# The first tile of parameters loaded and used ahead of the others in a four-layer trunk, the rest through GpSimd's queue

## The chip, the cores and the metric

One core of a Trainium2 chip. It has five engines that run beside each other: TensorE (PE; weight loads shown as PEld), VectorE (DVE), ScalarE (ACT), GpSimd (POOL) and SyncE (SP), and 16 DMA engines that they share. The metric is the device time of one execution in microseconds (us), the median over runs.

## The reference

A trunk of four layers over 256 latent tokens `x` and 256 context tokens `ctx`, 1024 wide, float32. Each layer is a mixer (HGRN2, RWKV-7, latent attention, HGRN2) and a convolutional GLU, each behind an RMS norm with a shift, a scale and a gate that come from a conditioning vector:

```python
silu_c, silu_cc = silu(c), silu(c_ctx)
for layer in range(4):
    mod_l = split(silu_c  @ w_mod[layer] + b_mod[layer], 6)     # w_mod[layer]: 1024 x 6144
    mod_c = split(silu_cc @ w_mod[layer] + b_mod[layer], 6)
    h_l = rmsnorm(x_l, norm1[layer]) * (1 + mod_l[1]) + mod_l[0]
    ...                                                          # mixer, gate, norm2, conv-GLU, gate
```

For layer 0 the first matmuls of the mixer need h, which needs shift and scale (the first third of the modulation), which need silu of `c` and `c_ctx`.

## The kernel before, in words

The kernel is written as a program of tiles. A planner of the tile framework, at build time, gives each engine its own fixed order: it goes by the order of the program, but an engine that its own estimate has free takes later work that is ready. On the chip each engine then works strictly in that order and waits on semaphores. Tiles of one tag share a fixed number of buffers.

`trunk` (line 2200) calls `consts` (line 253: identity for transposes, masks, cleared and cut out on POOL), then each layer. `hgrn` (line 609) opens the pools of layer 0 and calls `start` (line 341) as a generator: up to its first `yield` it does the work around the change, and what is left of it (`yield from steps`) is worked off behind the first projection (line 644).

What `start` does before, in the order of the program:

- `load_x` (line 329): SP loads four tiles of 128 tokens (`it`, 512 KB each, line 334); per 128 channels PE turns four 128x128 blocks into a PSUM bank of the tag `S` (two buffers; line 338), DVE copies it to `xT` (line 339).
- `params` (line 281): 790 rows of 128 values (all small vectors of the model) are gathered into seven `stage` tiles of 128 rows by 28 DMAs from ACT's queue (line 317). Rows 0 to 127, the first tile, are exactly `c`, `c_ctx`, `norm1`, layer 0's `b_mod` and `norm2`: five DMAs. The other 23 fill tiles 1 to 6 (the other layers' `b_mod`, `hg_lb` in tile 2, the convolution's weights, the RWKV vectors and so on). Then each tile is turned on PE (line 322) and copied by DVE into `prm` (line 323). A stage tile is one of the 16 buffers of the tag `mraw` (line 625), which the `w_mod` tiles use too.
- `silu_c` (line 353): POOL clears `sc` (line 356), ACT applies silu to the columns of `c_ctx` and `c` (line 358; ACT loads a function table first).
- `lower_bounds` (line 570): a softmax over `hg_lb`, two Exp on ACT (lines 583, 584) and some ten small operations on DVE.
- `mod` (line 383): for each of three groups g, 32 `w_mod` tiles (128x512, 256 KB, SP, line 396), each multiplied with `sc` on PE (line 397, two instructions per tile, four row groups side by side in PSUM `at`); then a copy (`modev`, line 400), four transposes (line 403), and bias and norm gain on DVE (`mod_part`, lines 372 to 380). `start` takes five steps of it: all of the first group and the beginning of the second.

Behind it `norm_mod` (line 527) squares xT on ACT (line 508), adds three of the squares on POOL and others on DVE (line 512), sums over channels on PE (line 517), and makes h in pieces (DVE line 549, ACT line 551, DVE line 552). The projection loads `hg_w_in` in 512 KB tiles from SP (line 430, four buffers `wraw`), splits each into a high and a low part (ACT line 431, DVE line 432) and multiplies (lines 639 to 641).

DMAs from SP and ACT draw on one set of eight completion counters in the order planned: a DMA waits for the one that used its counter last. DMAs from POOL have eight of their own.

Of the kernel before, what the change touches and what calls it, by code (L numbers as in the profile page):

```python
# [122 lines left out]
class Jobs:  # L123
# [20 lines left out]
    def schedule(self, places, stage, lat, ordered, locks=(), eps=0.05):  # L144
# [48 lines left out]
        while len(order) < len(self.list):  # L193
            best = (math.inf,)
            for x in ready:
                t = start(x, best[0])
                if t is not None:
                    best = min(best, (math.floor(t / eps), x.place, x.index, t))
            x, t = self.list[best[2]], best[3]
            for y in x.takes:  # L200
                r = y["ring"]
                if r == ordered:
                    todo[int(x.pair)] -= 1
                if len(live[r]) >= self.rings[r]:
                    old = [i for i, o in enumerate(live[r]) if not o["left"]]
                    live[r][min(old, key=lambda i: live[r][i]["end"])] = y
                else:
                    live[r].append(y)
            end = ended(x, t) if x.engine == "PE" else t + x.cost
            free[x.engine] = end  # L210
            if x.engine == "Pool":
                port[0] = max(port[0], end)
            ready.remove(x)
            order.append(x)
            for y in x.takes + x.uses:
                y["left"] -= 1
                y["end"] = max(y["end"], end + x.lag)
            for y in x.then:
                y.at = max(y.at, end + x.lag + lat[x.engine, y.engine])
                y.need -= 1  # L220
                if not y.need:
                    ready.append(y)
# [3 lines left out]
class Trunk:  # L226
# [54 lines left out]
    def params(self, raw, psum):  # L281
        nc, a = self.nc, self.a
        rows = []

        def add(name, ap):
            rows.append((name, ap, ap.shape[0]))

        def flat(t):
            names = "abcd"[: len(t.shape)]
            f = t.rearrange(f"{' '.join(names)} -> ({' '.join(names)})") if len(t.shape) > 1 else t  # L290
            return f.rearrange("(r p) -> r p", p=P)

        add("c", flat(a["c"]))
        add("c_ctx", flat(a["c_ctx"]))
        add("norm1", flat(a["norm1"]))
        add("b_mod0", flat(a["b_mod"][0]))
        add("norm2", flat(a["norm2"]))
        for l in range(1, DEPTH):
            add(f"b_mod{l}", flat(a["b_mod"][l]))
        for n in ("hg_lb", "hg_norm", "ffn_conv", "ffn_conv_b", "rw_mu", "rw_w0", "rw_a0", "rw_k_k", "rw_k_a",  # L300
                  "rw_r_k", "rw_ln_w", "rw_ln_b", "mla_q_norm", "mla_kv_norm", "norm_f"):
            add(n, flat(a[n]))
        total = sum(r for _, _, r in rows)
        ntile = -(-total // P)
        self.prm = self.cst.tile([P, ntile * P], F32, name="prm")
        self.off = {}
        stage = [raw()[:, :P] for i in range(ntile)]
        if total % P:
            nc.vector.memset(stage[-1], 0.0)
        pos = 0  # L310
        for name, ap, r in rows:
            self.off[name] = pos
            done = 0
            while done < r:
                t, o = divmod(pos, P)
                n = min(P - o, r - done)
                nc.scalar.dma_start(out=stage[t][o:o + n, :], in_=ap[done:done + n, :])
                done += n
                pos += n
        for i in range(ntile):  # L320
            ps = psum()
            nc.tensor.transpose(ps[:, :P], stage[i], self.ident)
            nc.vector.tensor_copy(self.prm[:, i * P:(i + 1) * P], ps[:, :P])

    def col(self, name, i=0, n=1):
        o = self.off[name] + i
        return self.prm[:, o:o + n]
# [12 lines left out]

    def start(self, l, raw, xs, psum1, psum2):

        self.load_x(xs, psum2)
        self.params(raw, psum2)
        self.silu_c()
        self.lower_bounds()
        steps = self.mod(l, raw, psum1)
        for _ in range(5):
            next(steps)
        yield  # L350
        yield from steps

# [101 lines left out]
    def mm3(self, ps, wh, wl, xh, xl, start, stop):  # L454
        nc = self.nc
        nc.tensor.matmul(ps, lhsT=wh, rhs=xh, start=start, stop=False)  # L456
        nc.tensor.matmul(ps, lhsT=wh, rhs=xl, start=False, stop=False)  # L457
        nc.tensor.matmul(ps, lhsT=wl, rhs=xh, start=False, stop=stop)  # L458
# [1783 lines left out]
```

## Time and profile before

| | us |
|---|---|
| median of 3 runs (3150.14 to 3155.94) | 3151.34 |
| the profiled execution | 3154.18 |
| its span, first to last instruction | 3152.4 |
| TensorE busy in it | 2875.8 |

All stretches and times below are counted from the span's start. A busy time is the time in which an engine has an instruction; a row of a timeline may merge several instructions of one group (x26), and ends with the idle time before it and what ended that. "ACTq" and "SPq" are the queues of these engines, with the DMAs that they issue.

### The profile page before, as it was taken

Reading aid. Unit: us, or ns where it says so; the run is one execution under the profiler, and the core shown is the slowest. Engines: PE = TensorE matmul, PEld = TensorE weight load, DVE = VectorE, ACT = ScalarE, POOL = GpSimd, SP = SyncE. Lnnn points to the kernel's source line nnn. Section 1 sums busy time; section 2 is a strip of 40 time slices with the busy share of each in tenths; the row PEclk is TensorE's granted clock in tenths of the full one; section 3 lists DMA queues with packets and bytes.
Section 4 is the critical chain, followed back from the end, with each engine's and each line's share of the span. In section 5 each row is a group of like instructions: output and inputs, shape, how many; then the busy total and the mean of one; then the engine's idle time right before and its main releaser. Section 6 shows DMA issues by size and latency. Waiting matters only on the chain. (4 is left out here: it accounts for less than half of the span.)

```text
span 3152.4 us, 52606 instructions
## 1 busy us (share of the span) xinstructions
PE 2875.8 (91%) x20861; PEld 2292.2 (73%) x20861; DVE 1767.0 (56%) x3113; ACT 1391.1 (44%) x2642; POOL 552.2 (18%) x727
## 2 busy tenths in 40 slices
PE   7999999999787787788879999899899999999898
PEld 4588877778575556666658888776578887888898
DVE  4278765445573346866564444466554344488765
ACT  3266643334442145665543223345433233577544
POOL 1023322222442133444310000000000000123000
PEclk9999989999888888988779999899999998999999
DMA  8622168886756865666553332210123332332554
GB/s 282 197 68 68 52 220 269 282 283 221 223 178 200 235 194 156 172 173 182 166 169 94 100 94 91 76 41 30 54 80 101 94 94 80 87 94 77 155 185 127
DMA packets 475336, 452.70 MB, mean 144 GB/s; under 512 B 98492, under 2 KB 415826, under 8 KB 474962
## 3 DMA queue, kind: packets, MB, share of 16 engines
q1 hardware_dynamic: 458352, 398.27, 41.3%
q0 software_dynamic: 15360, 50.34, 4.8%
q8 instruction: 164, 2.69, 0.4%
q10 hardware_dynamic: 1378, 0.73, 0.1%
q14 instruction: 82, 0.67, 0.1%
HBM read 392.64 MB, written 56.10 MB: 142 GB/s over the span
## 5 line engine op out<-in xcount | busy, mean ns | idle before, releaser
L457 PE MATMUL mm<-hl,whi 128*128 128x512 f32 (+1 forms) x2024 | 744.9, 368 | 10.9 <-DVE hl L552 10.9
L456 PE MATMUL mm<-hh,whi 128*128 128x512 f32 (+1 forms) x2024 | 744.8, 373 | 10.3 <-ACT hh L551 6.9
L458 PE MATMUL mm<-hh,wlo 128*128 128x512 f32 (+1 forms) x2024 | 742.4, 368 | 0.0
L432 DVE TENSOR_TENSOR wlo<-wraw,whi 128x1024 fp32r<-128x1024 f32 (+1 forms) x392 | 464.7, 1188 | 428.9 <-ACT whi L431 415.6
L431 ACT CAST whi<-wraw 128x1024 fp32r<-128x1024 f32 (+1 forms) x392 | 395.9, 1013 | 554.0 <-PE mm L457 489.6
L456 PEld LDWEIGHTS mm<-hh,whi 128*128 128x128 f32 x2024 | 386.2, 192 | 91.1 <-issue 10.8
L457 PEld LDWEIGHTS mm<-hl,whi 128*128 128x128 f32 x2024 | 386.0, 191 | 79.2 <-DVE hl L552 14.4
L458 PEld LDWEIGHTS mm<-hh,wlo 128*128 128x128 f32 x2024 | 385.6, 191 | 66.1 <-issue 6.1
L456 PE MATMUL mm<-uh,whi 128*128 128x512 f32 (+1 forms) x704 | 255.2, 363 | 0.0
L457 PE MATMUL mm<-ul,whi 128*128 128x512 f32 (+1 forms) x704 | 255.1, 363 | 0.0
L458 PE MATMUL mm<-uh,wlo 128*128 128x512 f32 (+1 forms) x704 | 254.2, 363 | 0.0
L512 POOL TENSOR_TENSOR t<-t,t 128x512 f32<-128x512 f32 (+1 forms) x27 | 35.2, 1305 | 868.1 <-ACT t L508 866.8
L456 PEld LDWEIGHTS mm<-uh,whi 128*128 128x128 f32 x704 | 132.8, 189 | 24.1 <-issue 2.5
L457 PEld LDWEIGHTS mm<-ul,whi 128*128 128x128 f32 x704 | 132.9, 189 | 20.3
L458 PEld LDWEIGHTS mm<-uh,wlo 128*128 128x128 f32 x704 | 132.5, 189 | 20.6
L449 DVE TENSOR_TENSOR plo<-praw,phi 128x512 fp32r<-128x512 f32 x64 | 45.3, 709 | 171.4 <-ACT phi L448 171.3
L448 ACT CAST phi<-praw 128x512 fp32r<-128x512 f32 x64 | 39.8, 622 | 216.3 <-DMA praw<-in_rw_w_rkv_dram 119.7
L2128 DVE SCALAR_TENSOR_TENSOR t<-mm,prm,t 128x510 f32<-128x510 f32 (+1 forms) x88 | 60.0, 682 | 105.4 <-ACT t L2126 105.4
L566 DVE SCALAR_TENSOR_TENSOR xT<-mm,mod,xT 128x256 f32<-128x256 f32 x176 | 74.4, 478 | 67.2 <-PE mm L458 67.2
L2126 ACT ACTIVATE t<-mm,prm 128x512 f32<-128x512 f32 (+1 forms) x88 | 63.3, 719 | 108.2 <-PE mm L458 108.2
L725 POOL TENSOR_TENSOR t<-t 128x512 f32<-128x512 f32 x32 | 46.4, 1450 | 362.6 <-DVE t L715 319.3
L1889 PE MATMUL md<-mraw,sc 128*32 128x256 f32 x768 | 71.5, 449 | 29.6 <-DMA mraw<-in_w_mod_dram 29.3
(426 smaller groups left out, 5199.7 us busy)
## 6 DMA issues: line engine op xcount, KB each, us to landing
wraw<-in_ffn_w_in_dram SPq DMA_DIRECT2D x176, 512.0 KB
mraw<-in_w_mod_dram SPq DMA_DIRECT2D x192, 256.0 KB
mraw<-in_w_mod_dram SPq DMA_DIRECT2D x96, 512.0 KB
wraw<-in_hg_w_in_dram SPq DMA_DIRECT2D x80, 512.0 KB
wraw<-in_ffn_w_out_dram SPq DMA_DIRECT2D x80, 512.0 KB
ow<-preo SPq DMA_DIRECT2D x64, 256.0 KB
praw<-in_rw_w_rkv_dram POOLq DMA_DIRECT2D x48, 256.0 KB, 4.4
vw<-prev SPq DMA_DIRECT2D x32, 256.0 KB
```

The costliest lines, as they stand in the source:

```text
L431: nc.scalar.copy(h, r)
L432: nc.vector.tensor_tensor(out=w, in0=r, in1=h.bitcast(F32), op=ALU.subtract)
L448: nc.scalar.copy(hi, raw)
L449: nc.vector.tensor_tensor(out=lo, in0=raw, in1=hi.bitcast(F32), op=ALU.subtract)
L456: nc.tensor.matmul(ps, lhsT=wh, rhs=xh, start=start, stop=False)
L457: nc.tensor.matmul(ps, lhsT=wh, rhs=xl, start=False, stop=False)
L458: nc.tensor.matmul(ps, lhsT=wl, rhs=xh, start=False, stop=stop)
L566: nc.vector.scalar_tensor_tensor(out=self.xT[n][:, sl], in0=ps[:, sl], scalar=m[:, which * 8 + n, s:s + 1], in1=self.xT[n][:, sl], op0=ALU ...
L725: nc.gpsimd.tensor_tensor(out=c3(de), in0=b3[:, :, end:end + 1].to_broadcast([P, 8, 64]), in1=b3, op=ALU.subtract)
L1889: nc.tensor.matmul(g["ps"][32 * c:32 * c + 32, halves[f]], lhsT=self.sc[:, k, :], rhs=g["raw", u][:, c], start=k == 0 and f == 0, stop=k = ...
L2126: nc.scalar.activation(c[:, sl], pa[b][:, sl], AF.Identity, bias=self.prm[:, cb + j + b:cb + j + b + 1], scale=w[1])
L2128: nc.vector.scalar_tensor_tensor(out=c3[:, :, 1:], in0=p3[:, :, :255], scalar=w[0], in1=c3[:, :, 1:], op0=ALU.mult, op1=ALU.add)
```

## The change

Three edits. In `params`, a load whose rows lie in the first tile still goes out from ACT's queue, and every other from POOL's. `params` becomes a generator that stops once, behind the transpose and copy of the first tile. `start` calls it first, then `silu_c`, `load_x` and the five steps of `mod`, and only then lets `params` turn the other six tiles and does `lower_bounds`.

```diff
@@ params
-                nc.scalar.dma_start(out=stage[t][o:o + n, :], in_=ap[done:done + n, :])
+                (nc.gpsimd if t else nc.scalar).dma_start(out=stage[t][o:o + n, :], in_=ap[done:done + n, :])
...
         for i in range(ntile):
             ps = psum()
             nc.tensor.transpose(ps[:, :P], stage[i], self.ident)
             nc.vector.tensor_copy(self.prm[:, i * P:(i + 1) * P], ps[:, :P])
+            if not i:
+                yield
@@ start
+        rows = self.params(raw, psum2)
+        next(rows)
+        self.silu_c()
         self.load_x(xs, psum2)
-        self.params(raw, psum2)
-        self.silu_c()
-        self.lower_bounds()
         steps = self.mod(l, raw, psum1)
         for _ in range(5):
             next(steps)
+        for _ in rows:
+            pass
+        self.lower_bounds()
         yield
         yield from steps
```

## Rows read from the trace of the kernel before

**Rows 1.** The page, part 1: TensorE's busy time, share of the span, instructions.
```profile
PE 2875.8 (91%) x20861; PEld 2292.2 (73%) x20861; DVE 1767.0 (56%) x3113; ACT 1391.1 (44%) x2642; POOL 552.2 (18%) x727
```

**Rows 2.** Stretches: length, busy us (instructions) per engine, granted clock, DMA share, GB/s.
```profile
0.00:15.36 15.36, 7.64 (x31) 5.05 (x32) 4.68 (x9) 0.00 (x0) 4.52 (x21) 1.00 0.82 290
...
14.00:16.00 2.00, 1.87 (x11) 1.09 (x9) 1.78 (x4) 0.00 (x0) 0.00 (x0) 1.00 0.31 93
...
15.36:26.80 11.44, 2.38 (x10) 1.01 (x9) 2.89 (x11) 1.73 (x4) 0.00 (x0) 0.61 0.79 258
26.80:45.90 19.10, 17.72 (x91) 6.43 (x92) 9.26 (x18) 11.45 (x18) 4.17 (x3) 0.88 0.99 346
...
45.00:50.00 5.00, 2.74 (x17) 0.80 (x15) 1.44 (x6) 2.25 (x3) 0.00 (x0) 1.00 1.05 388
...
60.00:70.00 10.00, 10.00 (x45) 8.26 (x44) 4.24 (x7) 2.52 (x3) 0.00 (x0) 1.00 0.54 177
```

**Rows 3.** Timeline, 0 to 60 us: start, us, engine, line, what, idle before and releaser.
```profile
0.81 0.59 ACTq L317 DMA_DIRECT2D mraw<-in_c_dram  x1
...
3.06 0.32 ACTq L317 DMA_DIRECT2D mraw<-in_norm_dram  x1
...
4.97 6.12 ACTq L317 DMA_DIRECT2D mraw<-in_b_mod_dram  x4
...
24.62 0.45 PE L322 MATMUL S<-ident,mraw 128*128 128x128 f32 x1 [5.85 <-DMA mraw<-in_rw_ln_b_dram]
...
24.68 0.28 ACTq L317 DMA_DIRECT2D mraw<-in_norm_f_dram  x1
...
25.04 1.28 ACT L358 ACT_TABLE_LOAD   x1 [25.04 <-DMA mraw<-in_w_mod_dram]
...
25.11 0.29 DVE L323 COPY prm<-S 128x128 f32<-128x128 f32 x1 [6.00 <-PE S L322]
...
26.34 0.32 ACT L358 ACTIVATE sc<-prm 128x8 f32<-128x8 f32 x2
...
26.80 5.92 PE L397 MATMUL at<-mraw,sc 128*32 128x512 f32 x26 [1.73 <-ACT sc L358]
...
45.18 1.90 PE L397 MATMUL at<-mraw,sc 128*32 128x512 f32 x10
...
45.70 0.11 PEld L397 LDWEIGHTS at<-mraw,sc 128*32 128x32 f32 x1 [0.37 <-DMA mraw<-in_w_mod_dram]
...
50.18 0.50 PE L639 MATMUL mm<-whi,hh 128*128 128x512 f32 x1 [1.76 <-ACT hh L551]
```

**Rows 4.** Timeline of SP's own queue: start, us, what it issued.
```profile
4.93 4.50 SPq L430 DMA_DIRECT2D wraw<-in_hg_w_in_dram  x4
15.36 23.93 SPq L396 DMA_DIRECT2D mraw<-in_w_mod_dram  x32
```

**Rows 5.** Waits of SP's queue, 9.5 to 26.8 us: us in total, times, longest.
```profile
SPq L396 <- DMA mraw<-in_b_mod_dram: 5.9, 1, 5.9
SPq L396 <- DMA mraw<-in_ffn_conv_b_dram: 1.4, 1, 1.4
```

**Rows 6.** Line 317, the parameter loads: ns min/median/max, first and last start.
```profile
L317 ACTq DMA_DIRECT2D mraw<-in_b_mod_dram x5: 318/318/437, 2.1 to 10.8; - x5
```

**Rows 7.** GpSimd: line 447's DMA issues with their landing; timeline rows of lines 356 and 512.
```profile
L447 POOL DMA_DIRECT2D praw<-in_rw_w_rkv_dram x48: 543/543/737, 391.1 to 749.2; - x48
...
DMA to landing us min/median/max: 3.2/4.3/7.8
...
3.08 0.31 POOL L356 MEMSET sc<- 128x256 f32 x1
...
29.41 4.32 POOL L512 TENSOR_TENSOR t<-t,t 128x512 f32<-128x512 f32 x3 [24.04 <-ACT t L508]
```

**Rows 8.** DMA queues, 0 to 60 us: ACT's queue, packets, MB, share of 16 engines.
```profile
q10 hardware_dynamic: 1090, 0.41, 2.5%
```

**Rows 9.** Timeline of TensorE: line 397's matmuls at the full clock.
```profile
99.86 3.64 PE L397 MATMUL at<-mraw,sc 128*32 128x512 f32 x32
```

## The prediction

> **What bounds the kernel now.** I began with the page's head [rows 1]: TensorE (PE) is busy for 91% of the span, so the change, which touches only the first 60 us, can win no more than the time in which PE there waits. The table of stretches [rows 2] says how much that is: from 60 us on PE is busy for 10.00 of 10 us, and nothing later is tied to the clock on the wall, so what the first stage gains or loses shifts all that follows. Up to 45.9 us PE is busy for 27.7 us in sum, and much of that is waiting inside a chain.
>
> The timeline [rows 3] gives the chain. ACT, as a queue, issues 28 small parameter loads from 0.81 to 24.96 us; only behind the last of them come silu's table load (25.04) and silu (26.34), and the first matmul of the modulation starts at 26.80. The last matmuls of its first group start at 45.18 and end at 47.08 (the weights at 45.70 still waited for a `w_mod` transfer), and the first projection matmul starts at 50.18. Two things can set that end: silu's late start, or the arrival of the 32 `w_mod` tiles. The DMA column [rows 2] decides for the second: 290 GB/s on average up to 15.36 us, 258 up to 26.8, 346 up to 45.9, and 388 only behind that. In one stretch, 14 to 16 us, it is 93. The stream is broken in the middle and full at the end, so the hole in it is what can be won.
>
> The hole's cause is on SP's own queue [rows 4]. SP issues x, then four `hg_w_in` tiles until 9.43 us, and the first `w_mod` tile only at 15.36, though nine of the sixteen `mraw` buffers are free. The waits [rows 5] name a parameter load from ACT's queue: 5.9 us for `b_mod`, 1.4 for `ffn_conv_b`. These two queues hold each other up: SP's tile reuses a completion counter of an ACT load, and ACT's loads wait in turn (one run of `b_mod` issues is spread over 6.12 us [rows 3]).
>
> **The change, part by part.**
>
> *Five loads stay on ACT, 23 go to POOL.* In ACT's queue 0.28 to 0.59 us per load go, and with them the waits between: the fifth load was issued at 3.06 us [rows 3], so ACT is free at 3.4 instead of 24.96. The last `b_mod` load was issued at 10.8 [rows 6] and SP's wait for it ended at 15.36, some 4.5 us; so tile 0 is complete at about 7.9. One transpose and one copy (0.45 and 0.29 us), the table load of 1.28 and two silus in 0.32 [rows 3]: `sc` can be ready near 10 us.
>
> *POOL's queue.* A DMA issue on POOL took 0.543 us (median, 0.737 at most) and its 256 KB landed after 4.3 us, 7.8 at most [rows 7]. 23 x 0.543 = 12.5 us. Beginning behind the masks at 3.1 us, POOL is through at 15.6 (20 at 0.737); the last tile has landed by about 20 to 28, where before the last but one was turned at 24.62 [rows 3]. Two things queue behind these issues on POOL. The memset of `sc` (0.31 us, at 3.08 before) stands behind them in the program now; if it stays there, silu starts at 16 instead of 8. And the three additions of squares for the first norm (4.32 us, at 29.41 before [rows 7]) start at 16 to 20, still before their old place. PE's queue waits for both, with `w_mod` matmuls behind. I price this at nothing for the end, because the `w_mod` tiles themselves arrive only from 13 us on and ten of them fit into buffers; if that cover is gone (POOL later than 20 us) it costs us for us until the buffers' stock, 16 x 0.68 = 11 us, has been used up.
>
> The Trainium skill's page "DMA: Bandwidth & Descriptors" (section "SWDGE vs HWDGE vs iDMA") says that GpSimd writes its descriptors into SBUF rings and that VectorE in its two-port mode locks it out there, which speaks against loads on this queue while DVE copies x. The 0.543 to 0.737 us of [rows 7], taken in a kernel whose DVE is busy for 56% of the span [rows 1], show at most 0.2 us of that per load. By the page's rule POOL could be held up for as long as DVE copies x; by the rows it is at most 4.5 us over 23 loads, POOL's end at 20 us, and the sum does not move.
>
> *SP's stream.* With no ACT load behind the fifth, `w_mod` tile 0 need not wait for 15.36; it can go out right behind `hg_w_in`, at 9.4 to 10 us. From there the stream is bound by bytes. Ahead of the last tile of the group lie x 2.1 MB, `hg_w_in` 2.1 MB, parameters 0.41 MB [rows 8] and 32 x 0.262 = 8.39 MB, 13.0 MB in all. Transfers begin in earnest after 2.4 us (the stretch to 15.36 us moved 290 GB/s x 15.36 = 4.46 MB, at 385 GB/s 11.6 us of work; of the 3.8 us that remain 1.5 lie in the hole at 14 us). At 385 GB/s the last tile lands at 2.4 + 33.8 = 36.2. This rate is seen only when the stream runs with large loads alone [rows 2], the row from 45 us; at the 346 GB/s of the stretch 26.8 to 45.9 the 8.5 MB from 15.36 on give 40. I take 37.5, nearer to the full rate, since what held the rate down to 346 was the buffers waiting for PE, which began late. Before, it landed at about 45.9. **Gain 8.4 us, bounds 5.9 and 9.7.** PE keeps up: 13 tiles took 5.92 us at half the clock, 0.46 us per tile, and 16 tiles 3.64 us at the full one, 0.23 [rows 3, 9], against 0.68 us that a tile takes to arrive.
>
> *Silu and the modulation ahead of x's transposes; the rest of the tiles and the lower bounds behind them.* On PE one transpose of 0.33 us goes ahead of 32; the six others move behind or between the modulation's matmuls. They can stop the stream if a tile from POOL is late where it stands; bounds 0 and 3 us, taken at 0 for the stock of buffers named above. The lower bounds' Exp on ACT waits for tile 2 from POOL (the seventh to eighth of 23 issues, near 8 us, landed by 16): no cost.
>
> *The granted clock.* It was 0.61 on average from 15.36 to 26.8, where PE was busy for 2.38 of 11.44 us, and 1.00 from 45 us on [rows 2]. If the thinner matmul stream brings PE to the projections at the lower of its two levels (1.2 and 2.4 GHz), some 5 us of work take 2.5 us more; bounds 0 and 2.5, taken at 0, because PE had its full clock at 45 to 50 us with only 2.74 of 5 us busy.
>
> Sum: the profiled execution's 3154.2 us less 8.4 is 3145.8. The median of the runs shown lies 2.8 us below that execution, so the median becomes 3151.3 - 8.4 = **3143**. What a measurement of this kernel can tell from no change is about 0.2%, 6.3 us.
>
> **The rivals.**
>
> 1. *SP fetches more projection weights first.* The order on SP is fixed at build time; four `hg_w_in` tiles already overtook `w_mod`. With ACT free, their casts come early and three buffers more come free; if these loads also overtake, 1.57 MB or 4.1 us lie ahead of the last `w_mod` tile. Gain 4.3: 3147. For it: it happened with four. Against: nothing but timing.
>
> 2. *Only the issue time is saved.* Here the stream keeps its old pace: `w_mod` still starts late and arrives at 346 GB/s: 15.36 + 2.4 + 24.2 = 42, against 45.9; with some small stop as in the trace the gain is 3: 3148. The skill's same page, "Issuing engines are not separate DMA queues", says that spreading issues over engines saves only the sequencer's time, the transfers sharing 16 DMA engines; for it speaks that the bytes stay the same, against it the 5.9 us that SP waited without transfers to make [rows 2, 5].
>
> 3. *`w_mod` overtakes `hg_w_in`.* 2.1 MB fewer lie ahead, 5.4 us; 1.4 go back for the first projection tile. Gain about 12: 3139.
>
> 4. *POOL becomes the bound (slower).* `sc` is cleared, or the sums of squares are made, behind 23 issues that go slower than 0.54 us. If PE starts the modulation at T, at most 16 tiles are there and 16 more take 10.9 us, with about 3 us for landing and matmuls: end T + 14. Before it was 47.1, so it breaks even at T = 33 and is 6.3 us slower (3158) from T = 39, at 1.6 us per issue. Against: 0.543 per issue, and even eight in flight at the worst landing, 23 / 8 x 7.8 us, give T = 26. For it: no row shows loads of 512-byte rows from POOL.
>
> 5. *The change doesn't do what it says*: the planner still puts silu or the matmuls behind the other tiles. Gain 0: 3151.
>
> **How the numbers follow.** Forecast 0.54 (of which 0.04 end under 6.3 us of gain), rival 1 0.13, rival 2 0.10, rival 3 0.08, rival 4 0.11, rival 5 0.04. Faster by over 0.2%: 0.50 + 0.08 = 0.58; within it: 0.04 + 0.13 + 0.10 + 0.04 = 0.31; slower: 0.11. The range runs from rival 3 with a little of the unknown ends (12 + 3 us: 3136) to rival 2 with most of the clock's bound (3 - 2 us: 3150); rivals 4 and 5 are left out. The forecast alone with its bounds: 3141 to 3148.
>
> **What would show it.** Right: silu near 10 to 16 us; SP's first `w_mod` issue near 10; over 360 GB/s in every stretch from 5 to 40 us; the first L639 matmul near 42; PE full from there. Wrong in its cause, if SP's first `w_mod` issue stays near 15 or seven `hg_w_in` loads stand ahead of it; wrong in its price for POOL, if the memset of `sc` or L512 on POOL starts after 20 us and PE waits for it; and if the first projection matmul comes 8 us earlier but the whole does not, the gain is given back later, in an order of work that has shifted.

## The result, and the profile after

The change makes the kernel slower. Its median is 3184.0 us (3181.09 to 3186.76, four runs) against 3153.64 us (3150.14 to 3163.82, four runs) for the kernel before in the same comparison: a ratio of 1.0106, 95% interval 1.0084 to 1.0128. The forecast was 3143 us, with a range of 3136 to 3150. The profiled execution took 3186.76 us, its span is 3184.7 us, 32.3 more than before.

Line numbers behind `params` have moved by 2, behind `start` by 5: silu is now L363 (L358 before), the w_mod matmul L402 (397), the copy `modev` L405 (400), the first projection L644 (639).

The head of the page answers to [rows 1]:

```profile
PE 2876.7 (90%) x20861; PEld 2298.9 (72%) x20861; DVE 1766.1 (55%) x3113; ACT 1478.1 (46%) x2710; POOL 564.8 (18%) x750
```

PE, PEld and DVE do the same work in the same time. ACT has 68 instructions and 87.0 us more (2710 against 2642, 1478.1 against 1391.1 us), POOL the 23 loads. The forecast had no term for ACT but the loads that it loses, so this one row says that something else has happened.

### The start: the hole filled, and little gained

The stretches of [rows 2] after the change (length, busy us and instructions of PE, PEld, DVE, ACT and POOL, granted clock, DMA share, GB/s):

```profile
14.00:16.00 2.00, 1.81 (x14) 1.22 (x13) 1.69 (x4) 1.56 (x4) 1.00 (x2) 1.00 1.01 336
15.36:26.80 11.44, 2.70 (x17) 1.39 (x19) 10.35 (x18) 8.57 (x14) 10.12 (x16) 0.74 1.05 380
26.80:45.90 19.10, 18.91 (x93) 6.56 (x93) 2.09 (x12) 2.97 (x5) 0.26 (x1) 0.89 0.99 349
```

The hole at 14 to 16 us is gone (336 GB/s where there were 93), and from 15.36 to 26.8 us 380 GB/s flow instead of 258. From 26.8 to 45.9 us the rate is 349 GB/s, about what it was (346). The timeline of the first 60 us, for [rows 3] (start, us, engine, line, what, idle before):

```profile
2.95 2.23 POOL L317 DMA_DIRECT2D mraw<-in_b_mod_dram  x4
...
18.91 0.51 POOL L317 DMA_DIRECT2D mraw<-in_norm_f_dram  x1 [0.47 <-DMA mraw<-in_rw_k_k_dram]
19.41 0.33 POOL L361 MEMSET sc<- 128x256 f32 x1
...
23.54 0.20 ACT L589 ACTIVATE lbt<-lbt 128x16 f32<-128x16 f32 x1
23.75 1.28 ACT L503 ACT_TABLE_LOAD   x1
...
25.04 1.28 ACT L363 ACT_TABLE_LOAD   x1
...
26.34 0.31 ACT L363 ACTIVATE sc<-prm 128x8 f32<-128x8 f32 x2
26.67 1.28 ACT L495 ACT_TABLE_LOAD   x1
...
26.75 5.74 PE L402 MATMUL at<-mraw,sc 128*32 128x512 f32 x28 [4.05 <-issue]
...
40.16 1.28 ACT L496 ACT_TABLE_LOAD   x1
...
45.78 0.58 ACT L405 COPY modev<-at 128x512 f32<-128x512 f32 x1 [4.11 <-PE at L402]
...
48.83 0.50 PE L644 MATMUL mm<-whi,hh 128*128 128x512 f32 x1 [0.38 <-ACT hh L556]
```

GpSimd issues its 23 loads from 2.95 to 19.42 us; behind them stands the clearing of `sc` (19.41, done at 19.74). Silu comes only at 26.34, as before (26.34), because other work stands ahead of it in ACT's order. The modulation begins at 26.75 (26.80), and the first projection matmul starts at 48.83 (50.18): 1.35 us are gained where 8.4 were forecast. SP's queue, for [rows 4], shows with what the filled stream was filled:

```profile
4.21 7.74 SPq L401 DMA_DIRECT2D mraw<-in_w_mod_dram  x9
12.03 0.40 SPq L435 DMA_DIRECT2D wraw<-in_hg_w_in_dram  x1
...
13.31 2.05 SPq L435 DMA_DIRECT2D wraw<-in_hg_w_in_dram  x3
...
20.84 2.87 SPq L435 DMA_DIRECT2D wraw<-in_hg_w_in_dram  x2
...
24.63 0.37 SPq L435 DMA_DIRECT2D wraw<-in_hg_w_in_dram  x1
25.35 33.92 SPq L401 DMA_DIRECT2D mraw<-in_w_mod_dram  x47
```

SP's first w_mod tile goes out at 4.21 us, not at 15.36. But seven `hg_w_in` loads (1 + 3 + 2 + 1) now go ahead of the last 18 w_mod tiles of the first group, which leave from 25.35 us on.

### The loss: function tables of ACT

The residual sum that ends the first stage of layer 0 (DVE, `xT` from `mm`) is one line in each kernel. The view of that line gives count, ns min/median/max, and its first and last start. Before the change:

```profile
L566 DVE SCALAR_TENSOR_TENSOR xT<-mm,mod,xT x176: 469/477/488, 389.4 to 3137.4; 128x256 f32<-128x256 f32 x176
```

and after:

```profile
L571 DVE SCALAR_TENSOR_TENSOR xT<-mm,mod,xT x176: 469/476/487, 422.8 to 3170.5; 128x256 f32<-128x256 f32 x176
```

33.4 us later at the first (422.8 against 389.4), 33.1 later at the last: the whole loss arises before 423 us, although the projection began 1.35 us early. ACT's groups by line show the 68 new instructions; before the change:

```profile
L498 ACT ACT_TABLE_LOAD x9 | 11.5, 1283 | 0.4 <-issue 0.3
...
L490 ACT ACT_TABLE_LOAD x1 | 1.3, 1283 | 0.0
L491 ACT ACT_TABLE_LOAD x1 | 1.3, 1283 | 0.0
```

and after it:

```profile
L604 ACT ACT_TABLE_LOAD x26 | 33.4, 1283 | 0.5
...
L668 ACT ACT_TABLE_LOAD x12 | 15.4, 1283 | 0.2
...
L503 ACT ACT_TABLE_LOAD x9 | 11.5, 1283 | 0.4 <-issue 0.3
L495 ACT ACT_TABLE_LOAD x9 | 11.5, 1283 | 0.2
L496 ACT ACT_TABLE_LOAD x9 | 11.5, 1283 | 0.2
L610 ACT ACT_TABLE_LOAD x9 | 11.5, 1283 | 0.2
```

They are loads of function tables, 1.283 us each, 87.2 us for 68. L495 and L496 are the Ln and the Exp of a norm's reciprocal root, L603, L604 and L610 the Exp, Ln and Exp that make the heads' silu. A piece of ACT's timeline in a head of layer 0 shows how they come:

```profile
187.79 1.28 ACT L495 ACT_TABLE_LOAD   x1
189.23 0.20 ACT L495 ACTIVATE rs<-rs 128x4 f32<-128x4 f32 x1 [0.16 <-DVE rs L494]
189.45 1.28 ACT L496 ACT_TABLE_LOAD   x1
190.74 0.21 ACT L496 ACTIVATE rs<-rs 128x4 f32<-128x4 f32 x1
...
191.32 0.60 ACT L603 ACTIVATE t<-mm 128x512 f32<-128x512 f32 x1
...
193.37 1.28 ACT L604 ACT_TABLE_LOAD   x1
194.67 1.15 ACT L604 ACTIVATE t<-t 128x512 f32<-128x512 f32 x2
```

Ln loads a table, Exp another, the next Ln the first again. Before, the same pair (then L490, L491) ran from 191.26 to 191.70 us with nothing between. The stretch from 160 us to the stage's end (columns as above), before the change:

```profile
160.00:393.00 233.00, 226.03 (x1993) 191.13 (x1993) 176.46 (x281) 147.88 (x291) 73.75 (x76) 1.00 0.22 63
```

and after:

```profile
160.00:426.00 266.00, 227.50 (x1944) 190.65 (x1943) 172.83 (x271) 218.91 (x344) 70.18 (x73) 0.95 0.18 53
```

PE is idle for 38.5 us where it was idle for 7.0, and its clock was granted at 0.95 where it was 1.00. And the waits of PE from 160 to 420 us (us in all, times, longest) name what it idles for. Before:

```profile
PE tr L749 <- DVE t L745: 6.8, 5, 1.6
```

and after:

```profile
PE tr L754 <- DVE t L750: 28.2, 8, 5.7
PE rd L529 <- DVE rs L499: 5.9, 4, 1.7
```

The heads' gates and norms go through ACT, DVE and PE in a chain, and loads in it leave PE waiting.

**Where the loads come from.** `norm_mod` begins with a call of `table`, which puts the load of a table that holds both Ln and Exp into ACT's order by hand:

```python
def table(self, name="natural_log_exp_and_others"):
    self.tc.keep_in_program_order(self.nc.scalar.preload_act_table_set(name))
```

This holds the load behind one instruction: the one that stands last before it on ACT in the program. Before the change that was the copy `modev`. The change puts `lower_bounds` behind the five steps of `mod`, so it is now the lower bounds' second Exp. In the planned order this Exp stands ahead of silu, since silu waits for `sc`, and `sc` for POOL's 23 issues. So the joint table is loaded at 23.75 us and replaced at 25.04 by silu's own, without one use. From then on, up to the next preload of the joint table at 454.39 us, a change from Ln to Exp or back finds the wrong table, and the load that the compiler puts in front of it brings one that lacks the other function.

The Trainium skill's page "ScalarE: Activation LUTs" (section "Table sets: the hidden batching unit") counts a Ln followed by an Exp as one load, because one set has both. The rows at 187.79 and 189.45 show two: here the rule held only where the joint set was already in place.

### The profile page after: what moved, and what is told of

Same layout as the page of the kernel before. It is cut to its first block, busy times and chain, and to the rows that moved or that the text cites. A ratio compares the mean times of both kernels' runs of the same rounds, so it can differ in the third digit from the quotient of the medians.

```text
span 3184.7 us, 52705 instructions
## 1 busy us (share of the span) xinstructions
PE 2876.7 (90%) x20861; PEld 2298.9 (72%) x20861; DVE 1766.1 (55%) x3113; ACT 1478.1 (46%) x2710; POOL 564.8 (18%) x750
## 4 chain that ended last, share of the span: by engine, by line
PE 70%; DVE 9%; ACT 8%; DMA 5%; issue 4%; POOL 2%; SPq 1%; DVEq 0%; ACTq 0%; POOLq 0%
PE mm L461 17%; PE mm L462 17%; PE mm L463 17%; DMA mraw<-in_w_mod_dram 2%; PE sc L2046 1%; PE at L402 1%; DVE t L554 1%; PE md L1894 1%; PE o L2078 1%; PE ax L1346 1%; ACT whi L436 1%; DMA vw<-prev 1%; DVE wlo L437 1%; ACT L604 1%; PE mm L646 1%
```

## The experiments

Each ratio is against the kernel before on the same chip, with its 95% interval; the table at the end has all runs beside one another.

**E2: the table loads alone.** The kernel before, without the one preload ahead of layer 0's first norm:

```diff
-        self.table()
+        if l or w:
+            self.table()
```

> The kernel before, without the preload of the joint table in layer 0's first norm; nothing of the change is in it. Theory (tables): the same loads by turns appear, 60 to 70 more, ACT is busy for 80 to 90 us more, and the time rises by 30 to 36 us to 3183 to 3190. Rivals (POOL, drift): no change beyond some 4 us, 3150 to 3158.

Measured: 1.0129 (1.0109 to 1.0149), 3197.58 against 3155.62 us. The loads by turns are back (26 loads on its line 600, 12 on 664, and so on), and the stage ends 41.7 us late. The rise of 40.7 us is more than the 30 to 36 that were expected. Nothing of the change is in this kernel, so the table loads alone cost at least what the change lost; the change had also won some 7 us elsewhere (see below).

**E1: the change with the preload held where it was.** The preload waits also for the first copy `modev`, in ACT's order only:

```diff
@@ mod
-            nc.scalar.copy(ev, ps)
+            i = nc.scalar.copy(ev, ps)
+            if g == 0 and l == 0:
+                self.ev0 = i
@@ table
-        self.tc.keep_in_program_order(self.nc.scalar.preload_act_table_set(name))
+        i = self.tc.keep_in_program_order(self.nc.scalar.preload_act_table_set(name))
+        if self.ev0 is not None:
+            self.tc.add_manual_dep(i.ins, self.ev0.ins.name, mybir.DependencyInfo(mybir.DependencyClass.NoSync, mybir.DependencyReason.DATA),
+                                   reason="table behind modev")
+            self.ev0 = None
```

> The changed kernel with one edge more: the preload of the joint Ln/Exp table for layer 0's first norm is kept behind the copy of modev, where it stood before the change; silu still comes late. Theory (tables): in the changed kernel ACT loaded the joint table at 23.75 us and silu's table at 25.04 threw it out, so that Ln and Exp in layer 0 load a table each time they alternate, 68 loads of 1.283 us more. Then here the 68 loads go, the span falls by 30 to 34 us to 3150 to 3154, and the first projection matmul stays near 48.8 us. Rival (POOL): the loss comes from the 23 loads and what is queued behind them on GpSimd; then 3180 to 3187 as in the changed kernel. Rival (drift): the order of layer 0 as a whole has shifted, by the modulation's steps; then also above 3175, with few table loads.

Measured: 0.9961 (0.9943 to 0.998). The preload stands at 48.73 us, and PE's busy time from 160 to 420 us is 252.49 us (253.03 before, 222.40 after the change). The head of the page has ACT's 2642 instructions of before again:

```profile
PE 2868.2 (91%) x20861; PEld 2290.6 (73%) x20861; DVE 1764.5 (56%) x3113; ACT 1390.1 (44%) x2642; POOL 562.9 (18%) x750
```

The loss is gone with this one edge, and the 23 loads on GpSimd, which are still there, did not cause it. Two things were not expected: the time is 12 us under the kernel before (3143.83, with 3150 to 3154 expected), and the first projection comes at 51.17 us, later than before. E11 asks where that gain lies.

**E3: the cause of silu's delay taken away.** The change, with `sc` made and cleared in `consts`, ahead of the 23 issues:

```diff
@@ consts
+        self.sc = self.cst.tile([P, KT, 32], F32, name="sc")
+        nc.gpsimd.memset(self.sc, 0.0)
@@ silu_c
-        self.sc = self.cst.tile([P, KT, 32], F32, name="sc")
-        nc.gpsimd.memset(self.sc, 0.0)
```

> The changed kernel with one move: sc is cleared on GpSimd ahead of everything else, so that the memset no longer stands behind the 23 loads. Theory (tables): silu then comes near 10 us, ahead of the joint table; no loads by turns, and the loss of 30 us goes. And the start: the modulation's matmuls are then paced by the w_mod tiles alone, the first projection matmul comes between 39 and 43 us in place of 48.8 (50.2 before), so 3141 to 3146, 8 to 10 us under the kernel before. Rival (POOL): the 23 loads are still there, so 3175 to 3185. Rival (the stream of transfers binds the start whatever silu does): first projection at 47 to 49 us and 3149 to 3153.

Measured: 0.9964 (0.9948 to 0.9981). ACT's timeline of this kernel:

```profile
14.14 0.31 ACT L363 ACTIVATE sc<-prm 128x8 f32<-128x8 f32 x2
...
28.55 1.28 ACT L588 ACT_TABLE_LOAD   x1
...
30.18 1.28 ACT L503 ACT_TABLE_LOAD   x1
```

Silu runs at 14.14 us, and the preload behind it at 30.18 stays. But the first projection comes at 49.87 us, only 0.3 earlier than before: silu early is not enough. The time that was expected (3141 to 3146) all but came, 3140.45, but not in the way that was expected. PE is busy for 14.73 us from 15 to 30 and for 15.00 from 30 to 45, the latter at a granted clock of 0.77.

**E8: `lower_bounds` put back ahead of `mod`**, with the other six tiles; the rest of the change stays:

```diff
-        steps = self.mod(l, raw, psum1)
-        for _ in range(5):
-            next(steps)
         for _ in rows:
             pass
         self.lower_bounds()
+        steps = self.mod(l, raw, psum1)
+        for _ in range(5):
+            next(steps)
```

> The changed kernel with one move in the program's order: the other tiles and the lower bounds stand ahead of the five steps of the modulation again, so that ACT's last instruction ahead of the norm is the copy of modev and not the lower bounds' Exp. Theory (tables): the preload goes back behind modev, the 68 loads vanish, ratio 0.994 to 0.998. Rival (something else of the new order costs the 30 us): above 1.005.

Measured: 0.9972 (0.9953 to 0.9991). Silu is as late as in the change (25.16 us), but the preload stands behind `modev` again (44.60), and there are no loads by turns.

**E6 and E5: half of the change each.** E6 is the change with all 28 loads on ACT; E5 is the kernel before with the 23 loads on GpSimd:

```diff
@@ E6, from the change
-                (nc.gpsimd if t else nc.scalar).dma_start(out=stage[t][o:o + n, :], in_=ap[done:done + n, :])
+                nc.scalar.dma_start(out=stage[t][o:o + n, :], in_=ap[done:done + n, :])
@@ E5, from before
-                nc.scalar.dma_start(out=stage[t][o:o + n, :], in_=ap[done:done + n, :])
+                (nc.gpsimd if t else nc.scalar).dma_start(out=stage[t][o:o + n, :], in_=ap[done:done + n, :])
```

> The changed kernel with all parameter loads on ACT's queue again: the new order alone, without GpSimd's queue. Theory (tables): silu stands behind the loads on ACT as before, at 25 to 26 us, and the lower bounds' Exp and the preload behind it, so the joint table survives: no loads by turns, 3148 to 3154. Rival (drift by the new order): 3175 or more. Rival (POOL): 3150 to 3156 as well, told apart by e1.

> The kernel before with one edit of the change: the 23 loads beyond the first tile go out from GpSimd's queue; the program's order is the old one, lower bounds ahead of the modulation. Theory (tables): the preload of the joint table is still kept behind the copy of modev, so no loads by turns, though silu is as late as in the changed kernel, near 25 us: ratio to before 0.994 to 0.998, like e1_pin. Rival (the loads on GpSimd cost by themselves): above 1.003.

Measured: E6 0.9994 (0.998 to 1.0007), E5 0.9977 (0.9962 to 0.9992). Neither half has loads by turns: in E6 silu (25.65) still runs before the lower bounds' Exp, in E5 silu is late but the preload hangs on `modev` (46.40). The loss needs both halves: silu late, by POOL, and the preload hung on something that does not wait for silu.

**E9 and E10: all w_mod tiles of the first group first.** On E3 and on E1, the first eight `hg_w_in` loads are put behind the 32nd w_mod load in SP's order, which takes rival 1 away:

```diff
@@ mod
-                    nc.sync.dma_start(out=t, in_=self.a["w_mod"][l][k * P:(k + 1) * P, c0:c0 + NT])
+                    i0 = nc.sync.dma_start(out=t, in_=self.a["w_mod"][l][k * P:(k + 1) * P, c0:c0 + NT])
+                    if l == 0 and g == 0:
+                        self.last = i0
@@ weights
-        nc.sync.dma_start(out=r, in_=ap)
+        i0 = nc.sync.dma_start(out=r, in_=ap)
+        if self.npin < 8:
+            self.npin += 1
+            self.tc.add_manual_dep(i0.ins, self.last.ins.name, mybir.DependencyInfo(mybir.DependencyClass.NoSync, mybir.DependencyReason.DATA),
+                                   reason="weights behind w_mod")
```

> e3_sc_early with the first eight weight loads kept behind the 32nd w_mod load on SP. In e3 silu came at 14.1 us and the transfers ran at 371 to 381 GB/s, yet the first projection matmul stayed at 49.9: six hg_w_in loads (3.1 MB) went out ahead of the last w_mod loads. Theory (bytes ahead of the last w_mod tile bind the start): with x 2.1, parameters 0.4 and w_mod 8.4 MB alone ahead, the last tile lands at 31 to 34 us and the first projection starts at 36 to 41; 8 to 12 us below e3, ratio to before 0.992 to 0.995. Rival (the norm's chain on PE, ACT and DVE binds): first projection at 45 us or later and the ratio of e3, 0.996.

> e1_pin with the same order of loads: silu late, near 25 us, w_mod ahead of the projection weights. Theory (bytes): sixteen buffers fill by 17 us and the transfers then stop until silu; end of the first group at about 26 + 14 = 40 us, first projection at 42 to 45, ratio 0.993 to 0.997. Rival (the norm's chain binds): first projection above 47 us, as e1_pin.

Measured: E9 0.9963 (0.9946 to 0.9981), E10 0.9988 (0.9967 to 1.0009). In E10 the first projection comes at 44.99 us, 5.2 earlier than before, but its first matmul with a low part waits until 51.51 for DVE, where the split of the `hg_w_in` tiles (cast from 43.49 us on) now stands behind the norm's pieces, and the stage ends only 4.5 us early; the whole, with a ratio above the 0.993 to 0.997 expected, cannot be told from no change. In E9 the copy `modev` comes at 40.40 (47.12 before), and the first projection still at 49.53. In between PE is busy with w_mod tiles of the second group for 5.2 of 9.1 us, at a granted clock of 0.53, besides the norm's last sums and the transposes:

```profile
43.34 2.12 PE L405 MATMUL at<-mraw,sc 128*32 128x512 f32 x4 [0.88 <-DVE mod L378]
...
46.43 3.17 PE L405 MATMUL at<-mraw,sc 128*32 128x512 f32 x10
```

And PE had been full before, from 11 to 41 us:

```profile
11.00:41.00 30.00, 29.06 (x121) 10.07 (x119) 11.65 (x28) 11.52 (x19) 11.25 (x20) 0.96 0.97 332
```

21.0 of these 29.06 us are w_mod matmuls, for 32 tiles.

**E11, E12: the tiles of one k together.** E1, E3, E5, E8 and E9 gain 7 to 12 us, of which the first projection shows 3 at most. The place is the rest of the modulation, from 47 to 180 us. In the timeline of PE before the change (start, us, line), beside the row of [rows 9]:

```profile
108.94 1.04 PE L397 MATMUL at<-mraw,sc 128*32 128x512 f32 x2
```

Sixteen tiles in a row take 3.64 us [rows 9], a single tile between dense matmuls 1.04. Before, in E6 and in E10 w_mod is busy for 35 to 36 us there, in these five for 29 to 31. To test it, the four tiles of one k (one block of 128 input channels), which go to four groups of 32 rows of PSUM side by side, are multiplied directly behind one another, the one loaded last first, on the kernel before (E11) and on E3 (E12). They are held together in the second and third group of layer 0 only:

```diff
-                    nc.tensor.matmul(ps[32 * i:32 * i + 32, :], lhsT=self.sc[:, k, :], rhs=t,
-                                     start=(k == 0), stop=(k == KT - 1), tile_position=(0, 32 * i))
+                    ts.append(t)
+                first = None
+                for i in reversed(range(4)):
+                    m = nc.tensor.matmul(ps[32 * i:32 * i + 32, :], lhsT=self.sc[:, k, :], rhs=ts[i],
+                                         start=(k == 0), stop=(k == KT - 1), tile_position=(0, 32 * i))
+                    if l == 0 and g and first is not None:
+                        self.tc.add_manual_dep(m.ins, first.ins.name, mybir.DependencyInfo(mybir.DependencyClass.NoSync, mybir.DependencyReason.DATA),
+                                               reason="four tiles together")
+                    first = first or m
```

> The kernel before, with one edit: behind the first group of the modulation of layer 0, the four w_mod tiles of one k are multiplied directly behind one another, beginning with the tile that was loaded last; loads and sums are the same. Theory A: a w_mod tile that stands alone between dense matmuls costs PE about 1.05 us against 0.23 us in a long run, and this is where the versions with the loads on GpSimd's queue gain their 10 us (w_mod matmuls busy from 47 to 180 us: 36.1 us before and with the new order alone, 29 to 31 with GpSimd's loads). Then this edit, with none of the change in it, brings the busy time of these matmuls from 36 to about 20 us, the residual sum that ends the layer's first stage comes 10 to 16 us earlier (389.4 before), and the ratio is 0.995 to 0.997. Theory B: the 1.05 us are only how the record puts the ends of these matmuls, PE loses nothing, and the gain of GpSimd's loads comes from elsewhere: busy time falls in the record, but the stage's end stays within 3 us and the ratio within 0.2% of 1.

> The version after the change with sc cleared first (which gave 0.9964), and the same edit of the modulation's matmuls as in the run beside it. Theory A: the lone tiles that this version still has (14, with w_mod matmuls busy for 31 us from 47 to 180 us) go too; 8 to 12 us on top of its 0.9964, so a ratio of 0.992 to 0.994. Theory B: it stays at 0.996 to 0.997.

Measured: E11 0.9949 (0.9928 to 0.997), E12 0.9935 (0.9909 to 0.996). PE's timeline in E11, and the stretch from 47 to 180 us for its w_mod matmuls alone (line 401 there; length, PE, PEld, clock, DMA share, GB/s). The timeline:

```profile
108.76 1.07 PE L401 MATMUL at<-mraw,sc 128*32 128x512 f32 x8
```

and the stretch:

```profile
47.00:180.00 133.00, 17.82 (x136) 3.26 (x128) 0.98 0.58 190
```

Four tiles (x8) take 1.07 us, as long as one alone; the busy time halves, and the stage ends 18.4 us earlier (10 to 16 were expected) with nothing of the change in the kernel. This shows that a lone w_mod tile costs PE real time. That the gain of GpSimd's loads lay there is not shown by a run of its own, but the third column of the table below supports it; why these versions have fewer lone tiles was not followed up.

**E14: E12 with w_mod first**, E9's edit, and with the four tiles of one k kept together in the first group too:

> The version with sc cleared first, the modulation's matmuls of one k kept together (as in the run that gave 0.9935), and the first eight hg_w_in loads put behind the 32nd w_mod tile on SP. Theory A: the forecast gain at the start was also eaten by PE, which was busy for 29.06 of 30 us from 11 to 41 us when the w_mod tiles went first, 21.0 of it on lone w_mod tiles; with these together (14.0 us in the run beside) the first group is through by about 35 us, the first projection matmul comes at 41 to 44 us against 47.97, and the ratio is 0.990 to 0.992. Theory B: the sums of squares for the norm, behind the modulation in PE's order, and a PE at its lower clock (0.53 granted from 30 to 45 us in the run beside) set the start: first projection at 46 to 49 us, ratio 0.993 to 0.995.

Measured: 0.9937 (0.9916 to 0.9958), no more than E12. The timeline of PE, and the stretch from 30 to 45 us for all engines. The timeline:

```profile
33.91 4.43 PE L537 MATMUL rd<-ones,t 128*128 128x1 f32 x20
38.27 1.93 PE L409 MATMUL at<-mraw,sc 128*32 128x512 f32 x8
...
45.64 0.80 PE L659 MATMUL mm<-whi,hh 128*128 128x512 f32 x1
```

and the stretch:

```profile
30.00:45.00 15.00, 14.22 (x66) 7.63 (x58) 6.40 (x15) 4.74 (x8) 0.00 (x0) 0.50 1.04 382
```

Theory B is the nearer one: the ratio lies in its range, and the first projection at 45.64 us just before its 46 to 49, not at 41 to 44. PE waited for tiles four times between 21 and 32 us (5.8 us in all), its granted clock is 0.50 from 30 to 45 us, the lower of its levels, and there the norm's 20 sums take 4.43 us (2.39 in E3) and four tiles 1.93 instead of 1.07.

All runs, in us: first projection matmul, w_mod matmuls on PE from 47 to 180 us, start of the residual sum less 389.4, and (ratio - 1) times the median of before in that comparison.

| kernel | first projection | w_mod, 47 to 180 | stage's end | whole, from the ratio |
|---|---|---|---|---|
| before | 50.18 | 36.11 | 0 | 0 |
| after | 48.83 | 30.16 | +33.4 | +33.4 |
| E2 | 49.06 | 35.45 | +41.7 | +40.7 |
| E1 | 51.17 | 31.22 | -6.7 | -12.3 |
| E3 | 49.87 | 30.97 | -7.2 | -11.4 |
| E5 | 48.85 | 30.14 | -9.0 | -7.3 |
| E6 | 48.62 | 36.20 | -1.6 | -1.9 |
| E8 | 47.05 | 29.07 | -10.8 | -8.8 |
| E9 | 49.53 | 29.57 | -11.0 | -11.7 |
| E10 | 44.99 | 34.94 | -4.5 | -3.8 |
| E11 | 51.18 | 17.82 | -18.4 | -16.1 |
| E12 | 47.97 | 16.33 | -24.1 | -20.5 |
| E14 | 45.64 | 15.78 | -25.9 | -19.9 |

What the first stage wins or loses reaches the end, within some 6 us. (In E8, E9 and E14, 4 to 8 of the 128 w_mod matmuls are missing from the records, so their third column is up to 2 us low. In E1 and E11 it holds about 1 us of the first group, which ended only at 48 us.) E12 and E14 are the best versions, equal within their intervals and 0.65 and 0.63% under the kernel before.

## Why the prediction was wrong

**The step that failed** is the last sentence of the part on silu and the modulation: "The lower bounds' Exp on ACT waits for tile 2 from POOL ...: no cost". It asked when that Exp would run (it ran at 23.42 us), not what hangs on its place in the program. The preload of the joint table hung on it. The prediction followed the table load ahead of silu and never asked which loads come behind it, though its rows showed one at 25.04. The term that was missing: 1.35 us of start and 5.95 us of w_mod (36.11 - 30.16) were gained and the stage still ended 33.4 us late, so by this sum the loads cost 40.7 us at the stage's end. Of these 31.5 are PE's idle time (38.5 - 7.0). The other 9 fit the lower clock (0.95 where it was 1.00), for PE is busy 1.5 us longer behind 160 us though it had some 7.3 us less left to do; no run separates the two. E2 has 41.7 + 1.1 + 0.7 = 43.5 by the same sum.

**What bounds the kernel** was read rightly in two points: the hole in the stream was real and closed, and what the first stage gains or loses did shift the rest. But of its two ends, silu or the arrival of the tiles, it chose one. With the hole closed and silu as late as before, the first projection came 1.35 us earlier; with silu early (E3) 0.3, with the w_mod tiles first and silu late (E10) 5.2, with both (E9) 0.65.

**ACT's queue**: right. ACT is free at 3.07 us (3.4 forecast), and SP's first w_mod issue comes even at 4.21 (9.4 to 10), since the plan put nine of them ahead of `hg_w_in`.

**POOL's queue** was priced well per load (0.50 to 0.56 us, median by tensor, against 0.543) and its end rightly put at 15.6 to 20 us (19.42). The Trainium skill's page "DMA: Bandwidth & Descriptors" (section "SWDGE vs HWDGE vs iDMA"), weighed there for VectorE's two-port mode, was taken to speak against these loads. While DVE copied x (10.75 to 17.08 us) they took 0.50 to 0.53 us each; the longest, 0.732, was the first, at 2.95, ahead of the copies. So nothing was held up, but no row tells whether these copies, which read a PSUM bank, ran in that mode, and the rule itself was not tested. "I price this at nothing for the end" failed: silu did not start at 16 but at 26.34, since the plan, which has silu late, puts the squares, three casts, the lower bounds and two table loads ahead of it on ACT. The cover that was named, w_mod tiles arriving only from 13 us on with ten buffers, hid it at the price of the gain: the end did not move back, and the 8.4 us did not come.

**SP's stream**: rival 1 came true, with seven `hg_w_in` loads ahead as it was described; its 4.3 us did not, since PE began the modulation no earlier than before; nor did they in E3, with six ahead, where PE began early and was full. E9, E10 and E14 put all of w_mod ahead of `hg_w_in`, more than the forecast assumed (four `hg_w_in` tiles ahead). The rate of over 360 GB/s "in every stretch" was reached up to 26.8 us only in part (336 from 14 to 16 us), and behind it 349 were measured.

**"PE keeps up"** failed too. With silu early (E3, E9) PE was full from about 14 us on. A w_mod tile between other matmuls costs 1.05 us and not 0.23 to 0.46 (in E9, 21.0 us for 32 tiles, 0.66 each, about the 0.68 that a tile takes to arrive), and the transposes of x come on top; only E12 and E14 have PE waiting for tiles again. And the clock, bounded at 0 to 2.5 us and taken at 0, held back the start of E14 together with the norm's sums. The bound itself was too low: 20 sums took 4.43 us at a granted clock of 0.50 and 2.39 in E3, so by that ratio 5 us of work would take some 4 us more (an estimate), not 2.5. The 8.4 us came at the start of no version that was run: the best first projection is 5.2 us early, in E10, where 4.5 us are left at the stage's end.

**The rivals and chances.** "Slower" had 0.11, all of it on rival 4, POOL as the bound. That mechanism did not decide: the modulation began at T = 26.75 where the rival breaks even at 33. The slowdown came by a way that was no rival. The last line of what would show it names "an order of work that has shifted", but for a first projection 8 us early, and it was 1.35 early here.

## What to carry to other kernels

Before moving a step, list what is ordered by hand relative to it (a preload of an ACT table above all), and ask which table is in place at every later use. Count the table loads of ACT by line in the profile after each change: 87 us of them beside a PE that is 90% busy cost some 41 us here by the sum above, through a chain that PE waits on. And where small matmuls can run side by side, keep them directly behind one another in the order, since one alone cost as much as four here (1.04 against 1.07 us).

## What the runs showed of the hardware that was not expected

- A table load took 1.283 us in every row, and the next instruction began 1.29 us after the load's start (189.45 to 190.74). The Trainium skill's page "ScalarE: Activation LUTs" (section "What ACT_TABLE_LOAD costs") gives the same 1283 ns, adds a drain and comes to about 2.66 us per switch. By the Trainium skill's figure the 68 loads would be 181 us of ACT, as an estimate; the rows show 87.2 us of loads, and ACT's busy time rose by 87.0.
- One w_mod tile of 128x512 with 32 columns of weights takes PE 1.04 us between dense matmuls, four of them in the four groups of 32 rows 1.07 us (E11), sixteen 3.64 us, all at the full clock.
- GpSimd issued the loads of 512-byte rows in 0.50 to 0.56 us each (median by tensor), about as it does 256 KB transfers (0.543).
